# A first MLP's second product with tokens on the partitions, and queries and keys in wider matmuls

## The chip, the cores and the metric

The kernel runs on one core of a Trainium2 chip. The metric is the device time of one execution of the whole program, in microseconds (us). One core has TensorE (PE in the profile, with its weight loads shown apart as PEld), VectorE (DVE), ScalarE (ACT), GpSimdE (POOL) and DMA queues started from SyncE (SP). The kernel before was timed in three executions: 753.31 to 753.59 us, median 753.58 us.

## The reference

The input is 256 tokens of width 1024 in fp32. Two layers follow one another, each a mixer and an MLP with residual adds and RMS norms; the change touches the first layer's MLP and the second layer's mixer.

```python
def sq_relu_mlp(xn, w1, w2):                 # w1 1024 x 4096, w2 4096 x 1024
    return jnp.square(jax.nn.relu(xn @ w1)) @ w2

def odd_mixer(xn, w_in, w_o, cos_f, sin_f):  # second layer's mixer
    hcat = (xn @ w_in).reshape(b, s, DIL_GROUPS, 3, DIL_HEADS, HEAD_DIM)   # 3 groups, 16 heads of 64
    q = apply_rope(hcat[:, :, :, 0], cos_f, sin_f)
    k = apply_rope(hcat[:, :, :, 1], cos_f, sin_f)
    v = hcat[:, :, :, 2]
    return dilated_attention(q, k, v) @ w_o

for layer in range(DEPTH):                   # DEPTH = 2: even mixer, then odd mixer
    xn = rms_norm(x, norm_mix[layer])
    x = x + mixer(xn, ...)
    x = x + sq_relu_mlp(rms_norm(x, norm_mlp[layer]), mlp_w1[layer], mlp_w2[layer])
return rms_norm(x, norm_final)
```

`dilated_attention` takes, for each head, a softmax over the keys of each of three dilated windows, and combines the three by their softmax denominators.

## The kernel before

**Split products.** Every fp32 product is made of three matmuls. A tensor is split into a high part in the type fp32r (a cast on ACT, line 179) and the rest (a subtraction on DVE, line 180), and `mm3` (lines 182 to 185) multiplies high by high, high by low and low by high into one PSUM bank. The weights come by DMA into `raw` (4 buffers of 1 MB), are cast to `whi` on ACT and reduced to `wlo` on DVE (3 buffers each), and are used as the matmul's stationary or moving operand. The product can be issued in another form with fewer matmuls: `xT[2]`, called `xp` after the change, holds the high and the low part of x beside each other, so one matmul of 512 columns (the weights' high part against both) and one of 256 columns (the weights' low part against x's high part) give all three terms, in two halves of a bank that are added afterwards. The first product of both MLPs ("up", lines 347 and 348) is done so: ACT copies one half of the bank out (line 351), and DVE adds the other (line 352).

**Stages.** Four phases follow one another: the even mixer to about 137 us, the first MLP (`mlp_between`) to 297 us, the odd mixer (`odd`) to about 566 us, the second MLP (`finish`) to the end. Between them `hand_over` adds the result to x (line 297), multiplies by the norm's gains and splits the sum again (`prepare`, lines 218 to 220), block by block of two of the eight 128-wide slices of the width, while PE finishes the next block. x lies with the width on the partitions and the tokens along the row.

**First MLP.** 16 chunks of the hidden width are worked off, "up" three chunks ahead of "down". The second product, "down" (line 377, `onto` at line 305), has the weights stationary and the 256 tokens of the hidden activations (`hh`, `hl`) moving; its result lies as x does, in four banks. The squared activations carry the norm's scale squared, so the result is multiplied by one number for each token; since tokens lie along the row here, `inverse_row` (line 254) spreads that number over all partitions with a matmul, and line 295 multiplies by it on DVE. The second MLP's "down" (lines 397 to 405) has the activations stationary and 512 columns of weights moving; its result lies with the tokens on the partitions, where the scale is one number for each partition.

**Odd mixer.** It works in eight units of two heads. For each unit PE computes three blocks of queries and keys (`qk_steps`, blocks b = 0, 1, 2, each with two halves f for q and k over eight slices of the width, 48 matmuls of 256 columns) and the values (48 matmuls of 384 columns, line 815). The rotary embedding follows each block (`rope`, lines 841 to 857): four copies on ACT that swap halves of the rows out of PSUM into `sw` (lines 844 and 845), a product of the PSUM bank with the cosines on DVE (`r`, line 847), a product of `sw` with the sines (line 848), and an add. The attention of the unit before runs beside these steps (`attend`, `weave`): scores, softmax (DVE, ACT, DVE, ACT, lines 893 to 897), transposes of the probabilities (line 904) with copies out (line 906), and the product with the values, `mix` (lines 914 to 919), whose results are split into `mixed` (line 921).

**Order.** Instructions are put in order by a scheduler from the program order and priorities; `tc.high_priority` moves a step ahead. Each engine works in its own order and waits for semaphores. PSUM has eight banks, four under the tag "acc", four under the tag "w".

Of the kernel before, what the change touches and what calls it, by code (L numbers as in the profile page):

```python
# [23 lines left out]
P = 128  # L24
D = 1024
# [19 lines left out]
def trunk(ctx, tc, a, out):  # L45
# [9 lines left out]
    def scratch(shape, name):  # L55

        n = int(np.prod(shape))
        v = work.tile([P, 512], F32, tag="scratch", name=name, bufs=12)[:, :n]
        if len(shape) == 2:
            v = v.rearrange("p (a b) -> p a b", b=shape[1])  # L60
        return v

    def pair_tile():


        z = act.tile([P, KT, 2, T], F32R, tag="pair", name="pair", bufs=1)
        return z[:, :, 0, :], z[:, :, 1, :], z
# [7 lines left out]
    def bank(tag):  # L75
        return ps.tile([P, 512], F32, tag=tag, name=tag)
# [136 lines left out]
    def two(z):  # L213
        return z.rearrange("p (f n) -> p f n", f=2)
# [36 lines left out]
        nc.vector.reciprocal(inv, inv)  # L251
        return inv

    def inverse_row(s):

        pr = bank("w")
        nc.tensor.matmul(pr[:, 0:T], mean, s[:, 0:T], start=True, stop=True)
        inv = work.tile([P, T], F32, tag="inv", name="inv", bufs=1)
        nc.vector.tensor_scalar(inv, pr[:, 0:T], EPS, None, ALU.add)
        nc.vector.reciprocal(inv, inv)  # L260
        return inv

    def diagonal(r, t):
        dg = work.tile([P, P], F32, tag="diag", name="diag")
        nc.vector.tensor_scalar(dg, ident, r[:, t:t + 1], float(D), ALU.mult, ALU.mult)
# [12 lines left out]
    def sum_tile():  # L278
        return work.tile([P, 2 * T], F32, tag="squares", name="squares", bufs=1)
# [2 lines left out]
        for s in steps:  # L282
            s()

    def hand_over(accs, last, n, scale=None):

        xT = pair_tile()
        s = sum_tile()
        for b in range(4):
            last[b]()  # L290
            v, acc = x[:, 2 * b:2 * b + 2, :], two(accs[b])
            with tc.high_priority(NORM_PRIO):
                if scale is not None:
                    scaled = scratch([2, T], "scaled")
                    nc.vector.tensor_tensor(scaled, acc, scale.unsqueeze(1).broadcast_to([P, 2, T]), op=ALU.mult)
                    acc = scaled
                nc.vector.tensor_tensor(v, acc, v, op=ALU.add)
                for f in zip(*(prepare(k, n, xT) for k in (2 * b, 2 * b + 1))):
                    run_all(f)
        return xT, s  # L300

    def open_accs():
# [28 lines left out]
    def mlp(mp, xT, s, invert, tail, make_down, beside=lambda j: None):  # L331
# [39 lines left out]
            beside(j)  # L371
        return accs, hs, inv, {j: weight() for j in tail}

    def mlp_between(mp, xT, s):
        def down(accs, hs):
            def step(j, w, f, fbs=range(8)):
                onto(accs, w, f * D, (ALL, slice(f * T, f * T + T)), hs[j], (j, f) == (0, 0), (j, f) == (15, 1), fbs)
            return step

        accs, hs, inv, w = mlp(mp, xT, s, lambda: inverse_row(s), range(14, 16), down)  # L380

        def last(b):
            for j in w:
                for f in range(2):
                    down(accs, hs)(j, w[j], f, (2 * b, 2 * b + 1))

        return accs, [lambda b=b: last(b) for b in range(4)], inv

    def finish(mp, xT, s):

        HALF = [slice(0, 512), slice(512, D)]
        g = mp.tile([P, D], F32, name="gain")
        nc.sync.dma_start(g, a["norm_final"].partition_broadcast(P))
        xt = mp.tile([P, NT, D], F32, name="xt")
        tail = range(13, 16)

        def mm(acc, hs, j, w, f, t, c0, c1, first, last):
            tk, c = slice(f * T + t * P, f * T + (t + 1) * P), slice(f * D + c0, f * D + c1)
            mm3(acc, hs[j][0][:, tk], hs[j][1][:, tk], w[0][:, c], w[1][:, c], first, last)

        def down(accs, hs):
            def step(j, w, f):
# [374 lines left out]


    def odd(op, xT, s):
        xh, xl, _ = xT  # L780
        cosT = op.tile([P, T], F32, name="cosT")
        sinT = op.tile([P, T], F32, name="sinT")
        mask = op.tile([P, NT, 384], F32, name="mask")
# [42 lines left out]
        def qk_steps(d):  # L826


            hold = {}

            def gemm(b, f, half):
                if f == 0 and half == 0:
                    hold["w"], hold["p"] = weight(), bank("acc")
                (wh, wl), pq = hold["w"], hold["p"]
                for k in range(4 * half, 4 * half + 4):
                    ws = slice((f * KT + k) * P, (f * KT + k + 1) * P)
                    mm3(pq[:, f * T:(f + 1) * T], wh[:, ws], wl[:, ws], xh[:, k, :], xl[:, k, :], k == 0, k == KT - 1)
                if f == 1 and half == 1:
                    rope(b, pq)

            def rope(b, pq):
                sw, r1 = scratch([512], "sw"), scratch([2, T], "r1")
                for r in range(0, P, 64):
                    nc.scalar.copy(sw[r:r + 32], pq[r + 32:r + 64])  # L844
                    nc.scalar.copy(sw[r + 32:r + 64], pq[r:r + 32])  # L845
                sw = sw.rearrange("p (f n) -> p f n", f=2)
                nc.vector.tensor_tensor(r1, pq.rearrange("p (f n) -> p f n", f=2), cosT.unsqueeze(1).broadcast_to([P, 2, T]), op=ALU.mult)  # L847
                nc.vector.tensor_tensor(sw, sw, sinT.unsqueeze(1).broadcast_to([P, 2, T]), op=ALU.mult)  # L848
                if b == 0:
# [21 lines left out]
        def attention(u, d):  # L871
# [36 lines left out]
            def mix(out_tag):  # L908
                pvo = [bank(out_tag) for _ in range(NT)]
                for i in range(NT):  # L910
                    for kk in range(NT):
                        for j in range(2):
                            cs = slice(64 * j, 64 * j + 64)
                            nc.tensor.matmul(pvo[i][cs, 0:P], d["v0"][:, kk, cs], turned[i, j][:, kk, :], start=kk == 0, stop=False)
                    for c in range(2):
                        qs = slice(64 * c, 64 * c + 64)
                        for j in range(2):
                            cs = slice(64 * j, 64 * j + 64)
                            nc.tensor.matmul(pvo[i][cs, qs], d["v12"][:, 2 * i + c, cs], turned[i, j][:, 2, qs], start=False, stop=c == 1)
                for i in range(NT):  # L920
                    split(*(z[:, u % 4, tok(i)] for z in mixed[u // 4]), pvo[i][:, 0:P])

            return scores, [lambda v=(i, j): turn(*v) for i in range(NT) for j in range(2)], mix

# [46 lines left out]
    accs, last = phase("even", even)  # L971
    xT, s = hand_over(accs, last, 1)
    accs, last, scale = phase("mlp0", mlp_between, xT, s)
    xT, s = hand_over(accs, last, 2, scale)
    accs, last = phase("odd", odd, xT, s)
    xT, s = hand_over(accs, last, 3)
    phase("mlp1", finish, xT, s)
# [94 lines left out]
```

## Time and profile before

| | |
|---|---|
| median of three executions | 753.58 us (753.31 to 753.59) |
| the profiled execution | 753.46 us |
| its span (first to last instruction) | 751.7 us |
| granted TensorE clock over the span | 0.998 of full speed |
| PE busy | 741.5 us, 99 % |
| PEld (weight loads) busy | 680.8 us, 91 % |
| DVE busy | 523.4 us, 70 % |
| ACT busy | 512.3 us, 68 % |
| POOL busy | 8.7 us, 1 % |
| DMA | 172 GB/s on average |

Matmuls are pipelined, so the length that a matmul's row shows is longer than the distance to the next one. What a group of matmuls costs is read from the distance of their starts. A row of the timeline gives start and length, engine, line, operation, the written and read names, and the shape as partitions x elements of a row; brackets hold idle time before it and what ended it. A row of groups gives count, busy time in us and the mean length in ns, then the idle time before them.

### The profile page before, as it was taken

The page shows a single profiled execution, that of the slowest core. Times are in us where ns is not written, and L with a number is a line of the kernel's source. Part 1 is how long each engine was busy: PE and PEld are TensorE (multiplying, and loading weights), DVE is VectorE, ACT ScalarE, POOL GpSimd, SP SyncE. Part 2 cuts the span into 40 slices and gives each one's busy share as a digit, 9 for nine tenths or more (in the row PEclk, how much of TensorE's full clock was granted, in tenths as well). Part 3 has the DMA queues.
Part 4 walks back from the last instruction along what each step waited for, and adds up shares of the span by engine and source line. Part 5 has one row for each costly group of instructions (what it writes and reads, how often), then busy time and mean ns, then how long its engine had stood idle before and what let it go on. Part 6 is the DMA issues. An engine that isn't in the chain of part 4 may idle for free.

```text
span 751.7 us, 13661 instructions
## 1 busy us (share of the span) xinstructions
PE 741.5 (99%) x5385; PEld 680.8 (91%) x5385; DVE 523.4 (70%) x1089; ACT 512.3 (68%) x1111; POOL 8.7 (1%) x20
## 2 busy tenths in 40 slices
PE   9999999999999999999999999999999999999996
PEld 6998998999999999999999999999898888888885
DVE  6778858866566557886777676776858765666664
ACT  6788866554454455898988989889866554554551
POOL 0100000000000001000000000000000000000000
PEclk9999999999999999999999999999999999999999
DMA  8772334555554554544443434534555455555501
GB/s 290 306 267 99 116 114 163 182 212 171 176 214 168 174 191 148 211 154 142 168 148 148 155 143 172 189 117 159 205 197 168 172 221 177 187 195 176 196 22 56
DMA packets 22097, 129.08 MB, mean 172 GB/s; under 512 B 2705, under 2 KB 3729, under 8 KB 9233
## 3 DMA queue, kind: packets, MB, share of 16 engines
q1 hardware_dynamic: 21888, 127.95, 48.0%
q8 instruction: 42, 0.69, 0.4%
q10 hardware_dynamic: 144, 0.26, 0.1%
q14 instruction: 23, 0.18, 0.1%
HBM read 127.16 MB, written 1.05 MB: 171 GB/s over the span
## 4 chain that ended last, share of the span: by engine, by line
PE 66%; ACT 17%; DVE 10%; issue 4%; DMA 2%; SPq 0%; POOL 0%; POOLq 0%
PE w L347 16%; PE acc L183 12%; PE acc L184 12%; PE acc L185 12%; PE w L348 8%; ACT whi L179 6%; DVE wlo L180 4%; ACT sw L845 3%; ACT sw L844 3%; ACT v L822 1%; DVE r L847 1%; ACT pp L895 1%; DVE sw L848 1%; DVE k L857 1%; DVE sn L893 1%
## 5 line engine op out<-in xcount | busy, mean ns | idle before, releaser
L180 DVE TENSOR_TENSOR wlo<-raw,whi 128x512 fp32r<-128x512 f32 (+3 forms) x487 | 306.6, 662 | 146.2 <-ACT whi L179 145.8
L179 ACT CAST whi<-raw 128x512 fp32r<-128x512 f32 (+3 forms) x487 | 265.8, 601 | 144.9 <-PE w L347 62.4
L347 PE MATMUL w<-pair,whi 128*128 128x512 f32 x512 | 182.3, 398 | 0.0
L348 PE MATMUL w<-pair,wlo 128*128 128x256 f32 x512 | 143.9, 281 | 0.0
L183 PE MATMUL acc<-pair,whi 128*128 128x256 f32 x432 | 123.5, 286 | 0.0
L185 PE MATMUL acc<-pair,wlo 128*128 128x256 f32 x432 | 120.2, 278 | 0.0
L184 PE MATMUL acc<-pair,whi 128*128 128x256 f32 x432 | 120.0, 278 | 0.0
L347 PEld LDWEIGHTS w<-pair,whi 128*128 128x128 f32 x512 | 96.4, 188 | 22.9
L348 PEld LDWEIGHTS w<-pair,wlo 128*128 128x128 f32 x512 | 96.2, 188 | 0.5
L183 PEld LDWEIGHTS acc<-pair,whi 128*128 128x128 f32 x432 | 81.2, 188 | 1.3 <-issue 0.3
L185 PEld LDWEIGHTS acc<-pair,wlo 128*128 128x128 f32 x432 | 81.5, 189 | 0.0
L184 PEld LDWEIGHTS acc<-pair,whi 128*128 128x128 f32 x432 | 81.3, 188 | 0.0
L184 PE MATMUL acc<-hl,whi 128*128 128x256 f32 x256 | 72.5, 283 | 0.0
L185 PE MATMUL acc<-hh,wlo 128*128 128x256 f32 x256 | 72.5, 283 | 0.0
L183 PE MATMUL acc<-hh,whi 128*128 128x256 f32 x256 | 72.4, 283 | 0.0
L183 PEld LDWEIGHTS acc<-hh,whi 128*128 128x128 f32 x256 | 49.1, 192 | 0.6
L185 PEld LDWEIGHTS acc<-hh,wlo 128*128 128x128 f32 x256 | 49.0, 192 | 0.0
L184 PEld LDWEIGHTS acc<-hl,whi 128*128 128x128 f32 x256 | 49.0, 191 | 0.0
L183 PE MATMUL acc<-whi,hh 128*128 128x512 f32 x122 | 48.0, 393 | 0.0
L185 PE MATMUL acc<-whi,hl 128*128 128x512 f32 x122 | 47.6, 390 | 0.0
L184 PE MATMUL acc<-wlo,hh 128*128 128x512 f32 x122 | 47.6, 390 | 0.0
L184 PE MATMUL acc<-wlo,pair 128*128 128x384 f32 x128 | 44.0, 344 | 1.2 <-DVE wlo L180 1.1
(215 smaller groups left out, 1267.0 us busy)
## 6 DMA issues: line engine op xcount, KB each, us to landing
raw<-in_w SPq DMA_DIRECT2D x64, 1024.0 KB, 4.8
raw<-in_w_oqk SPq DMA_DIRECT2D x24, 1024.0 KB, 4.8
raw<-in_w_ov SPq DMA_DIRECT2D x16, 768.0 KB, 4.2
raw<-in_w_qk SPq DMA_DIRECT2D x4, 1024.0 KB, 9.9
raw<-in_w_oe SPq DMA_DIRECT2D x4, 1024.0 KB, 5.0
raw<-in_w_oo SPq DMA_DIRECT2D x4, 1024.0 KB, 4.9
bias<-in_rpb SPq DMA_DIRECT2D x8, 256.0 KB, 3.8
raw<-in_w_v SPq DMA_DIRECT2D x2, 512.0 KB, 6.7
```

The source lines that it names most:

```text
L179: a = nc.scalar.copy(hi, src).ins
L180: return a, (eng or nc.vector).tensor_tensor(lo, src, hi.bitcast(F32), op=ALU.subtract).ins
L183: nc.tensor.matmul(o, sh, mh, start=first, stop=False)
L184: nc.tensor.matmul(o, sh, ml, start=False, stop=False)
L185: nc.tensor.matmul(o, sl, mh, start=False, stop=last)
L347: nc.tensor.matmul(two(pu[f]), w[0][:, c], xT[2][:, k], start=k == 0, stop=False)
L348: nc.tensor.matmul(pu[f][:, 0:T], w[1][:, c], xT[0][:, k, :], start=False, stop=k == KT - 1)
L822: nc.scalar.activation(d["v12"][64:P, 2 * i + c, :], pq[rows, 2 * P:3 * P], AF.Copy, scale=ri[rows])
L844: nc.scalar.copy(sw[r:r + 32], pq[r + 32:r + 64])
L845: nc.scalar.copy(sw[r + 32:r + 64], pq[r:r + 32])
L847: nc.vector.tensor_tensor(r1, pq.rearrange("p (f n) -> p f n", f=2), cosT.unsqueeze(1).broadcast_to([P, 2, T]), op=ALU.mult)
L848: nc.vector.tensor_tensor(sw, sw, sinT.unsqueeze(1).broadcast_to([P, 2, T]), op=ALU.mult)
```

## The change

The first MLP's "down" takes the second MLP's form (`down_tokens`): activations stationary, 512 columns of weights moving. Its result then has the tokens on the partitions; the next stage needs the width there. `hand_over_tokens` therefore scales each bank on the way out (the first 256 columns on ACT, the others on DVE, one number for each partition), turns the 16 squares of 128 x 128 by transposes on PE into banks of the tag "w", and then adds and splits as before. `inverse_row` goes, `inverse_columns` takes its place.

In the second layer, queries and keys take the form of the "up" product: per block and half f, eight matmuls of 512 columns and eight of 256 columns into a bank of their own, which a reduce on DVE (`tensor_reduce` over two elements) adds into the tile `qk32` in SBUF. The rotary embedding reads that tile in place of PSUM. The splits that take the mixed values out of PSUM get the priority of the norm steps.

```diff
@@ hand_over becomes two functions; join is what both do to a block
+    def join(b, o, n, xT):
+        v = x[:, 2 * b:2 * b + 2, :]
+        nc.vector.tensor_tensor(v, two(o), v, op=ALU.add)
+        for f in zip(*(prepare(k, n, xT) for k in (2 * b, 2 * b + 1))):
+            run_all(f)
...
-                if scale is not None:
-                    scaled = scratch([2, T], "scaled")
-                    nc.vector.tensor_tensor(scaled, acc, scale.unsqueeze(1).broadcast_to([P, 2, T]), op=ALU.mult)
-                    acc = scaled
...
+    def hand_over_tokens(accs, last, n, scale):
+        xT, s = pair_tile(), sum_tile()
+        ys = {}
+        def leave(h, t):
+            last(h, t)
+            acc, sc = accs[2 * t + h], column(scale, t)
+            with tc.high_priority(NORM_PRIO):
+                y = ys[h, t] = scratch([512], "y")
+                nc.scalar.activation(y[:, 0:T], acc[:, 0:T], AF.Copy, scale=sc)
+                nc.vector.tensor_scalar(y[:, T:2 * T], acc[:, T:2 * T], sc, None, ALU.mult)
+        def turn(h):
+            with tc.high_priority(NORM_PRIO):
+                for b in range(2):
+                    pt = bank("w")
+                    for k in range(2):
+                        for t in range(NT):
+                            c = (2 * b + k) * P
+                            nc.tensor.transpose(pt[:, k * T + t * P:k * T + (t + 1) * P], ys[h, t][:, c:c + P], ident)
+                    join(2 * h + b, pt, n, xT)
+        leave(0, 0)
+        leave(0, 1)
+        leave(1, 0)
+        turn(0)
+        leave(1, 1)
+        turn(1)
+        return xT, s
@@ mlp_between
-            def step(j, w, f, fbs=range(8)):
-                onto(accs, w, f * D, (ALL, slice(f * T, f * T + T)), hs[j], (j, f) == (0, 0), (j, f) == (15, 1), fbs)
+            def step(j, w, f):
+                for i in range(4):
+                    down_tokens(accs[i], hs, j, w, f, i // 2, i % 2 * 512, i % 2 * 512 + 512, (j, f) == (0, 0), False)
...
-        accs, hs, inv, w = mlp(mp, xT, s, lambda: inverse_row(s), range(14, 16), down)
+        accs, hs, inv, w = mlp(mp, xT, s, lambda: inverse_columns(s), range(14, 16), down)
@@ odd, qk_steps
-                    hold["w"], hold["p"] = weight(), bank("acc")
-                (wh, wl), pq = hold["w"], hold["p"]
+                    hold["w"], hold["q"] = weight(), scratch([2, T], "qk32")
+                if half == 0:
+                    hold["p"] = bank("acc")
+                (wh, wl), pq, q32 = hold["w"], hold["p"], hold["q"]
                 for k in range(4 * half, 4 * half + 4):
                     ws = slice((f * KT + k) * P, (f * KT + k + 1) * P)
-                    mm3(pq[:, f * T:(f + 1) * T], wh[:, ws], wl[:, ws], xh[:, k, :], xl[:, k, :], k == 0, k == KT - 1)
+                    nc.tensor.matmul(two(pq), wh[:, ws], xp[:, k], start=k == 0, stop=False)
+                    nc.tensor.matmul(pq[:, 0:T], wl[:, ws], xh[:, k, :], start=False, stop=k == KT - 1)
+                if half == 1:
+                    nc.vector.tensor_reduce(q32[:, f], pq.rearrange("p (h n) -> p n h", h=2), axis=mybir.AxisListType.X, op=ALU.add)
                 if f == 1 and half == 1:
-                    rope(b, pq)
+                    rope(b, q32.rearrange("p f n -> p (f n)"))
@@ odd, mix
-                for i in range(NT):
-                    split(*(z[:, u % 4, tok(i)] for z in mixed[u // 4]), pvo[i][:, 0:P])
+                with tc.high_priority(NORM_PRIO):
+                    for i in range(NT):
+                        split(*(z[:, u % 4, tok(i)] for z in mixed[u // 4]), pvo[i][:, 0:P])
...
-    xT, s = hand_over(accs, last, 2, scale)
+    xT, s = hand_over_tokens(accs, last, 2, scale)
```

Around the first block of a unit, DVE had this order before (`drz` is a reciprocal of the softmax, `obl`/`oal` the low part of mixed values, `r` and `sw` the rotary products, `q0l` the low part of the first block's queries and keys):

```order
L896 RECIPROCAL drz<-dz 128x1
L180 TENSOR_TENSOR oal<-acc,oah 128x128
L896 RECIPROCAL drz<-dz 128x1
L180 TENSOR_TENSOR wlo<-raw,whi 128x384
L847 TENSOR_TENSOR r_4889<-acc,cosT 128x512
L848 TENSOR_TENSOR sw<-sw,sinT 128x512
L180 TENSOR_TENSOR wlo<-raw,whi 128x384
L850 TENSOR_TENSOR r_4889<-r_4889,sw 128x512
L180 TENSOR_TENSOR wlo<-raw,whi 128x384 x2
L180 TENSOR_TENSOR q0l<-r_4889,q0h 128x512
```

With the change (line 868 is the reduce, line 937 the copy out of a transposed block of probabilities, before on ACT):

```order
L927 RECIPROCAL drz<-dz 128x1
L868 TENSOR_REDUCE qk_4662<-acc 128x256
L927 RECIPROCAL drz<-dz 128x1
L868 TENSOR_REDUCE qk_4662<-acc 128x256
L180 TENSOR_TENSOR wlo<-raw,whi 128x384
L878 TENSOR_TENSOR r_4782<-qk_4662,cosT 128x512
L180 TENSOR_TENSOR wlo<-raw,whi 128x384
L937 COPY pts<-w 128x384
L879 TENSOR_TENSOR sw<-sw,sinT 128x512
L868 TENSOR_REDUCE qk_4804<-acc 128x256
L881 TENSOR_TENSOR r_4782<-r_4782,sw 128x512
L180 TENSOR_TENSOR wlo<-raw,whi 128x384 x2
```

The two reduces of the block stand between and behind the last reciprocals of the softmax, ahead of the product with the cosines, which no longer reads PSUM; the next block's first reduce stands ahead of the add of this block, and two of a unit's four copies `pts` have come over from ACT.

At the end of the first MLP, PE had the last triples of the "down" product and then the first value products of the odd mixer (`pair` is the split x):

```order
L183 MATMUL acc_1853<-hh_3267,whi_3391 128x256
L184 MATMUL acc_1853<-hl_3268,whi_3391 128x256
L185 MATMUL acc_1853<-hh_3267,wlo_3392 128x256
L183 MATMUL acc_1853<-hh_3385,whi_3451 128x256
L184 MATMUL acc_1853<-hl_3386,whi_3451 128x256
L185 MATMUL acc_1853<-hh_3385,wlo_3452 128x256
L183 MATMUL acc_1853<-hh_3385,whi_3451 128x256
L184 MATMUL acc_1853<-hl_3386,whi_3451 128x256
```

With the change, the last 512-column matmul is followed by value products, between which transposes of the scaled result `y` stand:

```order
L185 MATMUL acc_1855<-whi_3116,hl_3075 128x512
L183 MATMUL acc_3280<-whi_3128,pair_3139 128x384
L184 MATMUL acc_3280<-wlo_3129,pair_3139 128x384
L185 MATMUL acc_3280<-whi_3128,pair_3139 128x384
L183 MATMUL acc_3280<-whi_3128,pair_3139 128x384
L184 MATMUL acc_3280<-wlo_3129,pair_3139 128x384
L312 MATMUL w_3221<-ident_84,y_3218 128x128
L312 MATMUL w_3221<-ident_84,y_3183 128x128
L312 MATMUL w_3221<-ident_84,y_3218 128x128
L185 MATMUL acc_3280<-whi_3128,pair_3139 128x384
L183 MATMUL acc_3280<-whi_3128,pair_3139 128x384
L312 MATMUL w_3231<-ident_84,y_3218 128x128
```

Sixteen transposes have come in on PE there; the scheduler puts them in singly four times and in threes four times, among the last "down" matmuls and the first 24 value products.

## Rows read from the trace of the kernel before

**Rows 1.** five units of the second layer: stretch, length, busy PE, PEld, DVE, ACT
```profile
352.08:381.79 29.71, 29.71 (x265) 29.38 (x265) 20.63 (x46) 27.30 (x59) 0.00 (x0) 1.00 0.45 160
...
442.54:473.21 30.67, 30.35 (x265) 29.25 (x265) 21.60 (x48) 27.32 (x59) 0.00 (x0) 1.00 0.43 155
...
sum 151.79, PE 150.72 PEld 146.47 DVE 106.41 ACT 136.59 POOL 0.00; mean PE 30.14 PEld 29.30 DVE 21.28 ACT 27.32 POOL 0.00
```

**Rows 2.** timeline of PE, first MLP: start, length, line, names, shape
```profile
200.30 0.28 PE L183 MATMUL acc<-hh,whi 128*128 128x256 f32 x1
...
206.05 0.40 PE L347 MATMUL w<-pair,whi 128*128 128x512 f32 x1
...
211.70 0.28 PE L183 MATMUL acc<-hh,whi 128*128 128x256 f32 x1
```

**Rows 3.** timeline of PE, second MLP's second product, first and last start
```profile
650.67 0.39 PE L183 MATMUL acc<-whi,hh 128*128 128x512 f32 x1
...
656.14 0.39 PE L347 MATMUL w<-pair,whi 128*128 128x512 f32 x1
```

**Rows 4.** timeline of PE inside one unit of the second layer
```profile
422.92 0.28 PE L184 MATMUL acc<-pair,whi 128*128 128x256 f32 x1
...
425.54 0.49 PE L904 MATMUL w<-ident,pp 128*128 128x128 f32 x3
...
425.99 0.28 PE L184 MATMUL acc<-pair,whi 128*128 128x256 f32 x1
...
429.99 0.28 PE L185 MATMUL acc<-pair,wlo 128*128 128x256 f32 x1
```

**Rows 5.** waits of one engine, 297 to 575 us: total, times, longest
```profile
PEld acc L184 <- DVE wlo L180: 3.7, 9, 0.6
...
PE w L192 <- DVE obl L180: 0.6, 1, 0.6
...
DVE r L847 <- ACT sw L845: 34.8, 24, 3.2
```

**Rows 6.** value products of two units (instructions on the cast weights): length, busy
```profile
373.38:381.79 8.41, 8.24 (x32) 5.94 (x33) 3.49 (x7) 4.04 (x8) 1.00 0.37 142
...
464.03:473.21 9.18, 8.26 (x32) 5.95 (x33) 2.91 (x6) 4.26 (x8) 1.00 0.49 187
```

**Rows 7.** timeline of ACT through one unit
```profile
425.93 0.58 ACT L844 COPY sw<-acc 32x512 f32<-32x512 f32 x1
...
432.14 0.58 ACT L844 COPY sw<-acc 32x512 f32<-32x512 f32 x1
...
436.89 0.58 ACT L844 COPY sw<-acc 32x512 f32<-32x512 f32 x1
...
444.08 0.36 ACT L821 ACTIVATE v<-acc,rstd 64x128 f32<-64x128 f32 x1 [2.12 <-DVE v L818]
...
456.59 0.58 ACT L844 COPY sw<-acc 32x512 f32<-32x512 f32 x1
```

**Rows 8.** groups by line and shape: count, busy us, mean ns, idle before
```profile
L844 ACT COPY sw<-acc 32x512 f32<-32x512 f32 x48 | 27.8, 578 | 0.9
...
L179 ACT CAST whi<-raw 128x512 fp32r<-128x512 f32 x408 | 229.7, 619 | 137.4 <-PE w L347 62.4 <-PE acc L184 29.9 <-issue 20.2
...
L906 ACT COPY pts<-w 128x384 f32<-128x384 f32 x31 | 14.6, 479 | 0.8 <-PE w L904 0.2
...
L847 DVE TENSOR_TENSOR r<-acc,cosT 128x512 f32<-128x512 f32 x24 | 16.6, 692 | 34.8 <-ACT sw L845 34.8
...
L352 DVE TENSOR_TENSOR u<-w,side 128x256 f32<-128x256 f32 x64 | 26.9, 420 | 3.9 <-ACT side L351 3.6
...
L260 DVE RECIPROCAL inv<-inv 128x256 f32<-128x256 f32 x1 | 1.7, 1745 | 0.0
```

**Rows 9.** timelines of PE and DVE at the hand-over into the second layer
```profile
297.38 0.33 PE L183 MATMUL acc<-whi,pair 128*128 128x384 f32 x1
...
301.08 0.87 DVE L220 SCALAR_TENSOR_TENSOR pair<-gx,pair 128x256 fp32r<-128x256 f32 x2
```

More of the change, by code (lines that the diff above doesn't have):

```diff
@@ L252, in inverse_columns @@
         return inv
[L254 to L261, printed above, removed]
     def diagonal(r, t):
@@ L283, in run_all, with hand_over @@
             s()
-    def hand_over(accs, last, n, scale=None):
-        xT = pair_tile()
-        s = sum_tile()
+    def join(b, o, n, xT):
[3 more added lines that the diff above has]
+            run_all(f)
+    def hand_over(accs, last, n):
+        xT, s = pair_tile(), sum_tile()
         for b in range(4):
             last[b]()
-            v, acc = x[:, 2 * b:2 * b + 2, :], two(accs[b])
             with tc.high_priority(NORM_PRIO):
-                if scale is not None:
-                    scaled = scratch([2, T], "scaled")
-                    nc.vector.tensor_tensor(scaled, acc, scale.unsqueeze(1).broadcast_to([P, 2, T]), op=ALU.mult)
-                    acc = scaled
-                nc.vector.tensor_tensor(v, acc, v, op=ALU.add)
-                for f in zip(*(prepare(k, n, xT) for k in (2 * b, 2 * b + 1))):
-                    run_all(f)
+                join(b, accs[b], n, xT)
+        return xT, s
+    def hand_over_tokens(accs, last, n, scale):
+        xT, s = pair_tile(), sum_tile()
+        ys = {}
[21 more added lines that the diff above has]
+        turn(1)
         return xT, s
@@ L372, in mlp, with down_tokens, last @@
         return accs, hs, inv, {j: weight() for j in tail}
+    HALF = [slice(0, 512), slice(512, D)]
+    def down_tokens(acc, hs, j, w, f, t, c0, c1, first, last):
+        tk, c = slice(f * T + t * P, f * T + (t + 1) * P), slice(f * D + c0, f * D + c1)
+        mm3(acc, hs[j][0][:, tk], hs[j][1][:, tk], w[0][:, c], w[1][:, c], first, last)
     def mlp_between(mp, xT, s):
         def down(accs, hs):
-            def step(j, w, f, fbs=range(8)):
-                onto(accs, w, f * D, (ALL, slice(f * T, f * T + T)), hs[j], (j, f) == (0, 0), (j, f) == (15, 1), fbs)
-            return step
-        accs, hs, inv, w = mlp(mp, xT, s, lambda: inverse_row(s), range(14, 16), down)
-        def last(b):
+            def step(j, w, f):
+                for i in range(4):
+                    down_tokens(accs[i], hs, j, w, f, i // 2, i % 2 * 512, i % 2 * 512 + 512, (j, f) == (0, 0), False)
+            return step
+        accs, hs, inv, w = mlp(mp, xT, s, lambda: inverse_columns(s), range(14, 16), down)
+        def last(h, t):
             for j in w:
                 for f in range(2):
-                    down(accs, hs)(j, w[j], f, (2 * b, 2 * b + 1))
-        return accs, [lambda b=b: last(b) for b in range(4)], inv
+                    down_tokens(accs[2 * t + h], hs, j, w[j], f, t, h * 512, h * 512 + 512, False, (j, f) == (15, 1))
+        return accs, last, inv
     def finish(mp, xT, s):
-        HALF = [slice(0, 512), slice(512, D)]
         g = mp.tile([P, D], F32, name="gain")
@@ L395, in finish @@
         tail = range(13, 16)
-        def mm(acc, hs, j, w, f, t, c0, c1, first, last):
-            tk, c = slice(f * T + t * P, f * T + (t + 1) * P), slice(f * D + c0, f * D + c1)
-            mm3(acc, hs[j][0][:, tk], hs[j][1][:, tk], w[0][:, c], w[1][:, c], first, last)
+        mm = down_tokens
         def down(accs, hs):
@@ L779, in odd @@
     def odd(op, xT, s):
-        xh, xl, _ = xT
+        xh, xl, xp = xT
         cosT = op.tile([P, T], F32, name="cosT")
```

## The prediction, made before the changed kernel ran

> **What bounds the kernel now.** I read the table of busy times first. PE is busy 741.5 of 751.7 us, so almost everything is the distance between starts of matmuls, and what I need is that distance for each shape that goes and each that comes. I read it from the timeline of PE. In the first MLP, the 48 matmuls of 256 columns between 200.30 and 206.05 take 5.75 us, 0.1198 us each; the 32 matmuls of the up product behind them, 16 pairs of 512 and 256 columns, take 5.65 us, 0.353 us a pair [rows 2]. In the second MLP, 24 matmuls of 512 columns take 5.47 us, 0.228 us each [rows 3]. In the second layer the query and key matmuls of 256 columns run at two rates: 23 intervals in the 2.62 us from 422.92, 0.1139 us each, and 34 in the 4.00 us from 425.99, 0.1176 us each; between them lie three transposes and one matmul of 256 columns in 0.45 us, which leaves 0.335 us for the three [rows 4].
>
> Then I read the busy times by unit, since there PE is not alone. The first steady unit is 29.71 us long and PE is busy in all of it; the later ones are 30.67 us with PE busy 30.35 [rows 1]. Their value products show why: 8.41 us in an early unit, 9.18 us in a late one, for the same 48 matmuls [rows 6]. The waits name the low part of the weights on DVE: 3.7 us in nine waits of PE's weight loads [rows 5]. ACT is busy 27.3 and DVE 21.6 us of the unit [rows 1], so neither is full, but they wait for one another: the cosine product on DVE waits 34.8 us for ACT's copies, over all blocks [rows 5]. The timeline of ACT shows the loop that results. The copies of one unit's three blocks start at 425.93, 432.14 and 436.89, the copies out of the values at 444.08, the next unit's first block at 456.59, 30.66 us later [rows 7]. That chain sets the late units; PE sets the early ones and the MLPs.
>
> **The change, part by part.**
>
> *First MLP's second product.* 768 matmuls of 256 columns become 384 of 512. By the distances above, 768 x 0.1198 = 92.0 us become 384 x 0.228 = 87.5 us: **-4.5 us**. The least gain is at the up product's rate, where two thirds of a pair's 0.353 are 0.235 a matmul: 90.4, -1.6 us. I take **-4.4**, as the second MLP issues this very form.
>
> *Hand-over.* 16 transposes come onto PE, in four threes at 0.335 us and four single ones. The three in rows 4 hold 0.24 us of start distances and some 0.095 us of restart, an estimate from where the next matmul starts; a single one is then 0.175 us. 4 x 0.335 + 4 x 0.175 = **+2.0 us**. The multiplication by the token's scale moves from DVE into the copies out, and the reciprocal over 256 columns (1.745 us, once, [rows 8]) becomes one over two; neither lies on PE's path, nothing. Before, the last split of this hand-over ended at 301.95, 4.57 us after the first value product at 297.38 [rows 9], and PE needs the second half of x after 24 value products, 24 x 0.175 = 4.2 us (rate from [rows 6]: 8.41 / 48). With eight transposes among them that is 5.2 us. The chain after the last matmul: y on ACT and then on DVE (about 0.42 us each, as the 256 columns from PSUM of [rows 8]), three transposes, then for two blocks an add (0.69) and two low parts (0.87 together in [rows 9]): 0.84 + 0.34 + 3.1 = 4.3 us. It fits; I take no stall. If the cover fails, it costs up to 1.5 us.
>
> *Queries and keys, PE.* A unit's 144 matmuls become 48 pairs. At the up product's rate 48 x 0.353 = 16.9 us. Before, with 98 of the 144 at the faster of the two rates and 46 at the slower, counted along the unit of rows 4, it was 98 x 0.1139 + 46 x 0.1176 = 16.6: **+0.4 us** a unit. So PE's own need is 29.7 + 0.4 = 30.1 us. If the pair ran at the faster rate, it would be 3 x 0.1139 = 0.342 and the need unchanged.
>
> *Queries and keys, DVE and ACT.* Each half of a block gets a reduce, six a unit. The trace has none. It reads 512 numbers a partition from PSUM and writes 256: below lies 0.42 us (an add of 256 from PSUM), beside it 0.692 us (the product over 512 from PSUM), above 1.745 us (a reciprocal of 256) [rows 8]. I take 0.69, the row with its amount of reading. The cosine product gets its operand from SBUF and no longer shares a bank with ACT's copies; before, it started after them. That takes 0.69 us off the loop where it stood behind the copies. Two of the four copies of transposed probabilities (0.479 us on ACT, [rows 8]) move to DVE. In all, on the loop: between the first and the second block's copies +0.25 (a reduce in, a product out of it); second to third nothing; from the third to the values -1.4 (product parallel to the copies, and the copy moved); to the next unit +0.55. From 30.66 that gives 30.1, and with ends of 29.3 and 30.5 for the copies' own time I take **30.3**.
>
> A bank is also held until its reduce is done, and there are six of them a unit now, out of four buffers that the mixed and the value products share. The first half of the third block takes the bank of the first block's first half. Its matmul comes about 5.5 us before the values, which start 21.5 us into the unit (464.03 after 442.54, [rows 1, 6]), so at 16.0. The reduce stands behind the softmax's reciprocals, ahead of the cosine product, and the copies before that started 14.05 us into the unit (456.59 after 442.54, [rows 1, 7]); with 0.7 us for the reduce that leaves 1.2 us. No wait.
>
> *Priority of the mixed values.* The casts come earlier on ACT, so the banks are free earlier. The single wait of the last product for them, 0.6 us [rows 5], goes: **-0.6**. What stands behind the casts on ACT is the softmax's scaling; two casts of 128 columns delay it by less than a `pts` copy each, once a unit; this is in the 30.3.
>
> *Second layer in all.* First two units' queries and keys: +0.8, as PE sets them. The five units, 151.79 us [rows 1]: the first becomes 30.1, four 30.3, 151.3, so -0.5. The last unit -0.1, the wait -0.6. Together **-0.4**.
>
> **Sum**: -4.4 + 2.0 - 0.4 = -2.8. The profiled execution took 753.46 us, its span 751.7 and 1.76 around it, which stays. 750.7; the median lies 0.12 above that execution: **750.8 us**.
>
> Two rules of the Trainium skill bear on this. Its page "TensorE: Matmul & The Clock Gate", section "Back-to-back issue gap", gives 262 cycles for 256 columns and 518 for 512 as the isolated gap, and says that the distance in a real stream is set by the load and the matmul together. By its gaps a pair would cost 0.325 us, against 0.353 in rows 2, so the trace does not agree for the pair; by the rule 48 pairs would be 15.6 us a unit. The page "VectorE: DVE Perf Modes", section "The TRN2 errata — SBUF-src ops pay a fixed extra latency per instruction", speaks against the change: it gives ScalarE 52 cycles more (43 ns, an estimate) for a copy from SBUF than for one from PSUM, and the rotary copies move from PSUM to SBUF. Rows 8 bear it out in sign.
>
> **The rivals.**
>
> *1. The pairs run at the faster rate.* For it: PE's weight loads are busy 29.38 of 29.71 us in a unit [rows 1], and the change takes 48 of a unit's loads away. Against: the up product has the very pair at 0.353 [rows 2]. The pair at 0.342 leaves PE's need at 29.7; the loop of 30.1 then decides. Five units 29.7 + 4 x 30.1 = 150.1, -1.7; the first two 0; the last -0.5; the wait -0.6: -2.8 and so 748.4 us; with the loop at 29.3 as well, 746.
>
> *2. The reduce is long (slower).* At 1.2 us, half-way to the bound, each reduce ahead of the cosine product lengthens the loop by 0.5 us at two or three places of the unit: 31.6. Five units 30.1 + 4 x 31.6 = 156.5, +4.7; first two and last +2.4; wait -0.6: +6.5, so 753.58 + 4.1 = 757.7 us. At the bound, DVE itself would be full: 21.6 + 6 x 1.745 + 2 x 0.48 = 33.0 us a unit, 764 us. It decides from about 0.9 us a reduce. For it: nothing in the trace bounds it from above but the reciprocal. Against: its reading is that of the row at 0.692.
>
> *3. The hand-over is exposed.* The last transposes stand five to ten value products behind the last matmul, and y needs two engines one after the other, as the cosine product waits for the copies of its bank [rows 5]. 1.5 us late gives 752.3 us.
>
> *4. The copies from SBUF are slower.* The nearest rows: 0.619 us for a cast of 512 columns from SBUF against 0.578 for the copy from PSUM [rows 8], 0.04 us, twelve of them a unit: +0.5. The loop is then 30.6. Five units 152.5, +0.7; the first two +0.8; the last +0.2; the wait -0.6: +1.1, and 752.3 us.
>
> **How the numbers follow.** Chances: forecast 0.45 (its own range 749 to 752.5, from the rate of the first part and the ends of the loop), rival 1 0.18, rival 2 0.12, rivals 3 and 4 0.13 and 0.12. The range 746 to 756.5 takes in rival 1 and the nearer part of rival 2 and leaves out less than 2 in 10. A measurement of this kernel tells 0.2 %, 1.5 us, from no change, so "faster" ends at 752.1. Faster: most of the forecast, rival 1, and a few of 3 and 4, 0.65. Same: most of 3 and 4, and the forecast's upper end, 0.23. Slower: rival 2, 0.12.
>
> **What would show it.** In the profile after: the 512-column matmuls of the first MLP 0.228 us apart; the pairs in the second layer at 0.353 or 0.342; a reduce of about 0.69 us; units of 30.3 us, the value products without the wait for low weights where PE sets the unit; no wait of PE for y, the transposed bank or a reduce's bank. Units above 30.7 us, or weight loads that wait longer for DVE than 3.7 us, would make the forecast wrong, as would 512-column matmuls at 0.235.

## The result and the profile after

The changed kernel takes 755.14 us (754.83 to 755.65, 16 runs); the kernel before took 753.62 us beside it (753.07 to 754.81). The ratio is 1.0018, interval 1.0011 to 1.0026: 1.5 us slower, where 2.8 us faster was forecast (750.8 us). The profiled execution took 755.53 us, its span 753.7. On the page PE's busy time is as before, its weight loads are fewer, and DVE has 32 us more:

```profile
PE 741.1 (98%) x4635; PEld 646.4 (86%) x4635; DVE 555.5 (74%) x1149; ACT 511.3 (68%) x1103; POOL 8.7 (1%) x20
```

The timeline of PE in the first MLP, in answer to [rows 2, 3]; 24 matmuls of 512 columns lie between the two starts, 5.47 us, 0.228 each, as the forecast took it:

```profile
198.50 0.39 PE L183 MATMUL acc<-whi,hh 128*128 128x512 f32 x1
...
203.97 0.39 PE L368 MATMUL w<-pair,whi 128*128 128x512 f32 x1
```

At the hand-over, in answer to [rows 9], the first value product starts at 294.20 us and not at 297.38. Threes of transposes stand among the value products, and queries start at 303.42 us, 2.28 us earlier than before (305.70). The forecast for the first MLP with its hand-over was -2.4:

```profile
294.20 0.34 PE L183 MATMUL acc<-whi,pair 128*128 128x384 f32 x1
...
295.13 0.55 PE L312 MATMUL w<-ident,y 128*128 128x128 f32 x3
...
303.42 0.39 PE L865 MATMUL acc<-pair,whi 128*128 128x512 f32 x1
```

So the time is lost behind 303 us. The busy times by unit (stretch, length, then PE, PEld, DVE, ACT, POOL with counts), in answer to [rows 1]:

```profile
350.74:380.76 30.02, 30.02 (x218) 27.44 (x217) 25.96 (x55) 25.74 (x54) 0.00 (x0) 1.00 0.40 142
...
442.41:473.71 31.30, 30.54 (x217) 27.42 (x217) 26.17 (x56) 26.73 (x57) 0.00 (x0) 1.00 0.43 152
...
sum 154.28, PE 151.89 PEld 137.13 DVE 129.68 ACT 132.68 POOL 0.00; mean PE 30.38 PEld 27.43 DVE 25.94 ACT 26.54 POOL 0.00
```

The first of these five units is PE's own length, 30.02 us (30.1 was forecast), and the second is 30.33 us long. The other three, the late units, are 31.3 us, where 30.67 was before and 30.3 forecast. The five together are 2.5 us longer than before, and the last unit's queries and keys (505.02 to 527.91 us, 22.89 us against 21.55) another 1.3. The stretch ahead of the five, with the first two units' queries and keys, is 0.9 us longer (0.8 was forecast), and the stretch behind 527.91 us 0.5 shorter; with the 2.28 us that gives the 2.0 us between the two spans. What PE shows is in its timeline in a late unit and in the waits of its weight loads between 294 and 577 us (total, times, longest):

```profile
449.34 0.39 PE L865 MATMUL acc<-pair,whi 128*128 128x512 f32 x1
...
451.46 0.40 PE L865 MATMUL acc<-pair,whi 128*128 128x512 f32 x1
...
452.68 0.50 PE L865 MATMUL acc<-pair,whi 128*128 128x512 f32 x1 [0.71 <-DVE oal L180]
```

```profile
PEld acc L865 <- DVE oal L180: 2.5, 3, 1.0
PEld acc L865 <- DVE obl L180: 2.1, 2, 1.0
```

Six pairs take 2.12 us, 0.353 each, as the forecast took it. Then the next half block waits for a PSUM bank that the mixed values of the unit before still hold (`oal`, `obl` are their low parts, and the bank is free when these have been taken out of it). The values no longer wait, 8.41 us, in answer to [rows 6]:

```profile
465.30:473.71 8.41, 8.23 (x32) 5.94 (x33) 3.06 (x5) 2.80 (x5) 1.00 0.45 168
```

That suggests a reading in which the bank is the cause. The timeline of ACT suggests another one, in answer to [rows 7]:

```profile
443.62 0.36 ACT L847 ACTIVATE v<-acc,rstd 64x128 f32<-64x128 f32 x1 [2.52 <-DVE v L844]
...
457.17 0.62 ACT L875 COPY sw<-qk 32x512 f32<-32x512 f32 x1
...
463.78 0.62 ACT L875 COPY sw<-qk 32x512 f32<-32x512 f32 x1 [0.28 <-DVE qk L868]
...
468.72 0.62 ACT L875 COPY sw<-qk 32x512 f32<-32x512 f32 x1 [0.47 <-DVE qk L868]
...
474.91 0.36 ACT L847 ACTIVATE v<-acc,rstd 64x128 f32<-64x128 f32 x1 [2.52 <-DVE v L844]
```

From the first block's copies to the second's it is 6.61 us, to the third's 4.94, from there to the values 6.19, and from the values to the next unit's first copies 13.55, where before it was 6.21, 4.75, 7.19 and 12.51. ACT's copies now wait for DVE's reduces. The groups that matter, in answer to [rows 8], DVE's wait for the copies, in answer to [rows 5] (34.8 us before), and the shares of the chain of waits over two late units, first after, then before (percent of 64 us; the lines of shares are cut at their end):

```profile
L868 DVE TENSOR_REDUCE qk<-acc 128x256 f32<-128x512 f32 x48 | 32.7, 683 | 0.3 <-PE acc L866 0.3
...
L875 ACT COPY sw<-qk 32x512 f32<-32x512 f32 x48 | 29.7, 618 | 5.2 <-DVE qk L868 4.7
...
L937 DVE COPY pts<-w 128x384 f32<-128x384 f32 x13 | 7.2, 551 | 0.0
```

```profile
DVE sw L879 <- ACT sw L876: 7.5, 14, 0.9
```

```profile
by line: DVE wlo L180 23.6%; ACT sw L876 7.8%; ACT sw L875 7.7%; DVE qk L868 7.5%; ACT whi L179 6.5%; DVE sw L879 6.4%; DVE sn L924 5.8%; DVE k L888 5.3%; issue 4.9%; ACT v L848 4.6%; ACT v L847 3.6%; ACT pp L928 2.7%; ACT pp L926 2.2%; DVE
```

```profile
by line: ACT whi L179 20.4%; DVE wlo L180 12.6%; ACT sw L845 9.2%; ACT sw L844 9.1%; issue 8.7%; DVE k L857 6.4%; ACT v L822 4.5%; DVE r L847 4.3%; ACT pp L895 4.1%; ACT v L821 4.1%; DVE sw L848 3.7%; ACT pts L906 3.0%; DVE sn L893 2.9%; AC
```

The chain goes round a late unit on the two engines alone; among its pieces there is none of PE, before or after. Added up piece by piece over one late unit, DVE had 10.2 of its 30.67 us and ACT 18.4 before; now DVE has 19.4 of 31.3 and ACT 11.2. This round of work, in which each engine waits for the other and which ends where the next unit's begins, is called the loop below. Theory 1 says that the banks cause the 31.3 us, theory 2 that this loop does and PE's wait is where PE catches up with it.

### The profile page after: what moved, and what is told of

Its sections match the earlier page's. It is cut to its first block, busy times and chain, and to the rows that moved or that the text cites. A ratio compares the mean times of both kernels' runs of the same rounds, so it can differ in the third digit from the quotient of the medians.

```text
span 753.7 us, 12208 instructions
## 1 busy us (share of the span) xinstructions
PE 741.1 (98%) x4635; PEld 646.4 (86%) x4635; DVE 555.5 (74%) x1149; ACT 511.3 (68%) x1103; POOL 8.7 (1%) x20
## 4 chain that ended last, share of the span: by engine, by line
PE 65%; DVE 16%; ACT 12%; DMA 3%; issue 3%; SPq 1%; POOL 0%; POOLq 0%; ACTq 0%
PE w L368 16%; PE acc L183 11%; PE acc L185 11%; PE acc L184 11%; PE w L369 8%; DVE wlo L180 6%; ACT sw L876 3%; ACT sw L875 2%; ACT whi L179 2%; DVE qk L868 2%; DVE sw L879 2%; PE acc L865 2%; DVE sn L924 1%; DVE k L888 1%; ACT v L848 1%
## 5 line engine op out<-in xcount | busy, mean ns | idle before, releaser
L865 PE MATMUL acc<-pair,whi 128*128 128x512 f32 x384 | 140.7, 405 | 3.1 <-DVE oal L180 1.4
L183 PE MATMUL acc<-whi,hh 128*128 128x512 f32 x250 | 98.1, 393 | 0.0
L185 PE MATMUL acc<-whi,hl 128*128 128x512 f32 x250 | 97.7, 391 | 0.0
L184 PE MATMUL acc<-wlo,hh 128*128 128x512 f32 x250 | 97.7, 391 | 0.0
L865 PEld LDWEIGHTS acc<-pair,whi 128*128 128x128 f32 x384 | 72.2, 188 | 21.9 <-DVE oal L180 2.5
L185 PEld LDWEIGHTS acc<-whi,hl 128*128 128x128 f32 x250 | 47.0, 188 | 9.9
L183 PEld LDWEIGHTS acc<-whi,hh 128*128 128x128 f32 x250 | 47.0, 188 | 9.9
L184 PEld LDWEIGHTS acc<-wlo,hh 128*128 128x128 f32 x250 | 47.0, 188 | 8.8
L183 PE MATMUL acc<-whi,pair 128*128 128x384 f32 x128 | 43.8, 342 | 0.0
L185 PE MATMUL acc<-whi,pair 128*128 128x384 f32 x128 | 43.1, 337 | 0.0
L875 ACT COPY sw<-qk 32x512 f32<-32x512 f32 x48 | 29.7, 618 | 5.2 <-DVE qk L868 4.7
L868 DVE TENSOR_REDUCE qk<-acc 128x256 f32<-128x512 f32 x48 | 32.7, 683 | 0.3 <-PE acc L866 0.3
```

Of the source, the lines that this page charges most:

```text
L183: nc.tensor.matmul(o, sh, mh, start=first, stop=False)
L184: nc.tensor.matmul(o, sh, ml, start=False, stop=False)
L185: nc.tensor.matmul(o, sl, mh, start=False, stop=last)
L865: nc.tensor.matmul(two(pq), wh[:, ws], xp[:, k], start=k == 0, stop=False)
L868: nc.vector.tensor_reduce(q32[:, f], pq.rearrange("p (h n) -> p n h", h=2), axis=mybir.AxisListType.X, op=ALU.add)
```

## The experiments

In each, the kernel before ran beside it on the same chip (753.2 to 753.4 us). Rows of stretches are to be read as those of the units above.

**The parts one at a time.** Each of two kernels has one part of the change: the first MLP with its hand-over, or the second layer's.

```diff
-    xT, s = hand_over(accs, last, 2, scale)
+    xT, s = hand_over_tokens(accs, last, 2, scale)     # and mlp_between as changed; odd as before
```

> Only the first MLP's second product by token and its hand-over; queries, keys and the mixed values' splits as before. In the trace of the change the second layer starts its value products 3.2 us earlier and its query products 2.3 us earlier than before. If the two parts of the change add up, this kernel is 2.3 us faster than the one before (751.3 us), and units of the second layer stay at 30.67 us. Rival: the loop of the second layer takes the gain back, because it starts with less slack; then it is within 1 us of the one before.

750.9 us, ratio 0.9967 (0.9955 to 0.9980).

> Only the second layer's part (pairs of matmuls, reduce, priority of the splits); first MLP as before. If the parts add up: +4.3 us, 757.9 us, with late units of 31.3 us and the same waits of PE for the mixed values' bank. Rival: the longer units come from the state that the new hand-over leaves behind; then units stay near 30.7 us and the time near 754 us.

757.8 us, ratio 1.0063 (1.0049 to 1.0076). One late unit of each:

```profile
439.54:470.21 30.67, 30.36 (x265) 29.30 (x265) 21.59 (x48) 27.34 (x59) 0.00 (x0) 1.00 0.45 156
```

```profile
444.20:475.50 31.30, 30.56 (x217) 27.42 (x217) 26.17 (x56) 26.73 (x57) 0.00 (x0) 1.00 0.44 152
```

That is -2.3 and +4.6 us; their sum, 2.3, differs from the whole change's 1.5 by less than the intervals, of about 1 us to either side each, can tell. The first part does what was forecast, and the second, forecast at -0.4, loses 4.6 by itself, whatever stands ahead of it.

**One bank for the mixed values.**

```diff
-                pvo = [bank(out_tag) for _ in range(NT)]
+                pv = bank(out_tag)
+                pvo = [pv[:, i * P:(i + 1) * P] for i in range(NT)]
```

> The change, but both mixed-value products of a unit go into one PSUM bank, so a unit takes nine banks of the four in turn and not ten; no work is added or taken away. Theory 1 (PSUM banks: PE waits 1.08 us a late unit for a bank that the mixed values hold, and that alone makes units 31.3 us): the wait goes or shrinks, units come to 30.2 us, 751 us. Theory 2 (VectorE and ScalarE form a loop of 31.3 us by themselves, since VectorE got 4.1 us of reduces a unit between ScalarE's copies; PE's wait for the bank is only where PE catches up with it): units stay at 31.3 us, the wait shows up at another place (the values' weights, the next unit's scores), 755 us.

761.18 us, ratio 1.0102 (1.0089 to 1.0116). A late unit, and all that PE's weight loads wait for in it:

```profile
442.51:474.10 31.59, 30.24 (x218) 27.38 (x218) 26.13 (x56) 26.85 (x57) 0.00 (x0) 1.00 0.45 150
```

```profile
PEld w L935 <- ACT pp L928: 1.7, 1, 1.7
PEld w L192 <- issue: 0.3, 1, 0.3
```

The wait for the bank is gone, the unit is no shorter, and PE waits at another place, for the softmax. Theory 1, by which the unit had to shrink with that wait, falls. The edit did not take away the wait alone, though: in the trace the splits of the mixed values stand behind further softmax steps on both engines, and the unit is 0.3 us longer. The further 5 us are lost behind the units: from the last unit's value products to the end it takes 231.0 us, against 225.8 in the change, with one stop of PE of 3.5 us (1.1 there) and a lower clock behind it (last section).

**A shorter reduce.** One half of the bank is copied and the sum of the two halves is left out.

```diff
-                    nc.vector.tensor_reduce(q32[:, f], pq.rearrange("p (h n) -> p n h", h=2), axis=mybir.AxisListType.X, op=ALU.add)
+                    nc.vector.tensor_scalar(q32[:, f], pq[:, 0:T], 1.0, None, ALU.mult)
```

> The change, but the reduce reads only one half of the bank (a copy of 256 columns, the sum of the two halves is left out), so VectorE does about 0.27 us less six times a unit, 1.6 us, and everything else is as in the change, banks too. Theory 2 (loop of VectorE and ScalarE): late units fall from 31.3 by most of the 1.6 us until PE's own 30.2 us bounds them, 750.5 to 752 us. Theory 1 (banks): the bank of the mixed values comes free at the same place in the order behind the softmax, units stay above 31 us, 754 to 755 us.

753.1 us, ratio 0.9998 (0.9989 to 1.0007); a late unit, the group in place of the reduce, and the chain's shares over that unit:

```profile
441.42:472.38 30.96, 30.27 (x217) 27.42 (x217) 24.60 (x56) 26.71 (x57) 0.00 (x0) 1.00 0.45 153
```

```profile
L868 DVE TENSOR_SCALAR qk<-acc 128x256 f32<-128x256 f32 x48 | 19.9, 416 | 0.3
```

```profile
by line: DVE wlo L180 23.2%; ACT sw L876 10.1%; ACT sw L875 10.1%; issue 7.8%; DVE sw L879 6.7%; ACT whi L179 6.7%; DVE sn L924 6.0%; ACT v L848 4.7%; DVE k L888 4.4%; ACT v L847 3.6%; DVE qk L868 3.3%; ACT pp L928 2.8%; ACT pp L926 2.3%; D
```

Neither number was met: 1.6 us less on DVE gave 0.35 us a unit. The chain shows where most of the rest went: ACT's rotary copies grew from 15.5 % of it (over the two units above) to 20.2, 5.0 to 6.3 us a unit, and the time in which no wait is seen (issue) from 4.9 to 7.8 %. In that part of the unit the two engines are nearly level, and most of what one gives, the other takes.

**The priority.** The splits of the mixed values without `tc.high_priority` in the change, and with it in the kernel that has the first MLP's part alone.

> The change without the priority of the mixed values' splits. The prediction gave the priority 0.6 us, once. Theory 1 (banks): the splits come later, PE waits longer for their bank, late units grow beyond 31.3 us, over 757 us. Theory 2 (loop of VectorE and ScalarE): the same work stands in another order on the two engines, a late unit changes by no more than 0.3 us either way, 754 to 757 us.

755.68 us, ratio 1.0035 (1.0021 to 1.0048); a late unit is 31.32 us long, though PE's weight loads now wait up to 1.4 us at a time for the bank, where it was 1.0:

```profile
443.18:474.50 31.32, 30.28 (x218) 27.43 (x218) 26.12 (x56) 26.73 (x57) 0.00 (x0) 1.00 0.43 151
```

That is what theory 2 expected. The pieces of the chain over this unit are 15.7 us of DVE and 14.9 of ACT, against 19.4 and 11.2 in the change, at the same length: two ways round that are nearly equally long.

> The first MLP's part and the priority of the mixed values' splits, queries and keys as before. By the prediction the priority is worth 0.6 us once: 750.3 us. By the loop: the splits' places on ScalarE and VectorE move by one or two instructions, 750.5 to 751.3 us.

751.78 us, ratio 0.9980 (0.9972 to 0.9989), a late unit 30.89 us. The 0.6 us were not gained. If anything the priority costs here, which is not shown: the interval overlaps that of 0.9967 without it.

**Part of the subtractions on GpSimd**, in the change and in the first MLP's part alone.

```diff
+        if odd_lo <= j < odd_hi and i == 3:
+            eng = nc.gpsimd
         return split(hi, lo, raw, eng)
```

> The change, but in the second layer the last of the four low-part subtractions of every weight chunk runs on GpSimd, which is idle there, so VectorE does 2.8 us less a unit (three of 0.6 us, two of 0.47 us). Theory 2 (loop): units fall from 31.3 to 30.2 to 30.6 us, near PE's own need, 750.5 to 752.5 us. Theory 1 (banks): the mixed values' splits stand behind the same softmax on ScalarE, so the wait for their bank stays and units stay above 31 us, 754 to 755 us. A third way: GpSimd's subtraction is so slow, or slows VectorE so much, that weights come late; then PE waits for them, and it is slower than 755 us.

772.17 us, ratio 1.0256 (1.0242 to 1.0270).

> The first MLP's part of the change alone, with the same subtractions on GpSimd. Without them it took 750.9 us, with late units of 30.67 us and a loop of ScalarE and VectorE in which ScalarE has 18 and VectorE 10 us. Theory 2: units fall toward PE's 29.7 us, 747 to 750 us. If VectorE's work does not count in this loop, since ScalarE's does: 750.5 to 751 us. If GpSimd is too slow: over 751 us.

765.28 us, ratio 1.0160 (1.0146 to 1.0174). Both went the third way, so they say nothing on the theories. The groups in the first of the two kernels:

```profile
L184 POOL TENSOR_TENSOR wlo<-raw,whi 128x512 fp32r<-128x512 f32 x24 | 44.3, 1846 | 94.7 <-ACT whi L183 63.6 <-DVE v L848 24.0 <-PE acc L869 4.5
```

```profile
L885 DVE TENSOR_TENSOR r<-r,sw 128x512 f32<-128x512 f32 x8 | 11.1, 1383 | 0.2
```

GpSimd takes 1.25 to 1.83 us for what DVE does in 0.69 (the mean of 1.85 has the first, of 6.16 us, in it), and the add on DVE that falls beside it takes 1.38 us as a mean of eight in place of 0.68.

**Work taken off ScalarE.** Two copies for the rotary swap in place of four, which exchange the two heads and leave out the exchange of the halves within each; or the four as DMAs.

```diff
-                    nc.scalar.copy(sw[r:r + 32], pq[r + 32:r + 64])
-                    nc.scalar.copy(sw[r + 32:r + 64], pq[r:r + 32])
+                    nc.scalar.copy(sw[r:r + 64], pq[64 - r:P - r])
```

> The change, but ScalarE makes two copies of 64 rows for each block's rotary swap and not four of 32 rows (the two heads are swapped instead of the halves within a head), 2 x 0.62 us less a block, 3.7 us less a unit; banks, reduces and their order stay. Theory 2 (loop of ScalarE and VectorE): the copies are 4.96 us of the loop in the trace; without half of them it falls below PE's own need and units are 30.2 us, PE's wait for the mixed values' bank goes, 750.5 to 751.5 us. Theory 1 (too few banks in themselves): the bank of the mixed values is released behind the softmax as before, the wait of about 0.9 us stays and units are 31 us or more, 754.5 to 755.5 us.

747.86 us, ratio 0.9930 (0.9916 to 0.9943). A late unit, the longest waits of PE's weight loads from 303 to 570 us, and two groups:

```profile
440.23:470.25 30.02, 30.02 (x218) 27.43 (x218) 25.15 (x54) 24.00 (x54) 0.00 (x0) 1.00 0.46 158
```

```profile
PEld w L192 <- issue: 2.0, 8, 0.3
PEld w L263 <- DVE diag L256: 0.4, 1, 0.4
```

```profile
L875 ACT COPY sw<-qk 64x512 f32<-64x512 f32 x48 | 29.8, 620 | 0.9
L936 ACT COPY pts<-w 128x384 f32<-128x384 f32 x31 | 14.6, 475 | 2.3 <-PE w L934 2.2
```

A copy of 64 rows takes as long as one of 32 (0.620 and 0.618 us), so the edit takes 3.7 us a unit off ACT. Banks and reduces are those of the change. The scheduler did more than the edit, however: the two copies `pts` that the change had put on DVE are on ACT again, and both engines' order is another, so that ACT has 2.7 us less a unit and DVE 1.0 (25.15 and 26.17). With less work on the two engines the unit is PE's own 30.02 us, and no wait for the bank is left. Theory 2 is shown from this side, for the two engines together; what the copies alone did is not separated from the rest. The time lies below what was expected, which came from the units alone: from the end of the seventh unit's values to the end it is 245.8 us against 248.7 in the change, another 2.9.

> The change, but the rotary swap, which now reads SBUF, is made by four small DMAs a block from SyncE's queue instead of four copies on ScalarE: 7.4 us less a unit on ScalarE. Theory 2: units at PE's 30.2 us, 750.4 us, if the DMAs land within about 3 us. Rival: their landing, or the weight loads that wait behind them in SyncE's queue, takes the copies' place in the loop, and units stay above 31 us, 755 us or more.

747.41 us, ratio 0.9922 (0.9909 to 0.9934), with the full computation: units of 30.02 us, ACT at 20.19 us of them, and the DMAs land in 2.0 us. Here too the `pts` copies are all on ACT again, and DVE has 25.14 us:

```profile
440.38:470.40 30.02, 30.02 (x218) 27.43 (x217) 25.14 (x54) 20.19 (x48) 0.00 (x0) 1.00 0.56 184
```

```profile
sw<-qk SPq DMA_DIRECT2D x96, 64.0 KB, 2.0
```

**The old form without the loop.** The first MLP's part alone, queries and keys as before, with two or all four of a unit's copies `pts` on VectorE (the line shown is the one for all four).

```diff
-                nc.any.tensor_copy(out=pts, in_=pt[:, 0:384].rearrange("p (b n) -> p b n", b=3))
+                nc.vector.tensor_copy(out=pts, in_=pt[:, 0:384].rearrange("p (b n) -> p b n", b=3))
```

> The first MLP's part alone, and two of a unit's four copies of transposed probabilities on VectorE instead of ScalarE (0.95 us less on ScalarE, in whose part of the old loop they stand with 0.95 us). By theory 2, applied to the kernel before (18.4 us of its loop are ScalarE's), late units fall from 30.67 to 29.7 to 30.1 us: 747.5 to 749.5 us. If the copies only go from one side of the loop to the other: 750.5 to 751 us.

748.18 us, ratio 0.9931 (0.9919 to 0.9943); late units are 29.7, then 30.26 us.

> As the one before it, with all four copies on VectorE. By theory 2 late units at PE's 29.7 us, 747 to 748.5 us, unless VectorE becomes the longer side, then 750 to 752 us.

745.91 us, ratio 0.9900 (0.9887 to 0.9914): the fastest of these kernels, 7.5 us below the kernel before. Units are PE's 29.70 us to the last:

```profile
438.71:468.41 29.70, 29.70 (x266) 29.37 (x265) 23.27 (x53) 25.62 (x55) 0.00 (x0) 1.00 0.45 161
```

## Why the prediction was wrong

**The step that failed** is "Queries and keys, DVE and ACT", the sum over the loop: "From 30.66 that gives 30.1 [...] I take 30.3". It measured 31.3, and the prediction's own sign, units above 30.7 us, came. The terms, each as forecast and then as the timeline of ACT shows it: first to second block +0.25 and +0.40; second to third nothing and +0.19; third to the values -1.4 and -1.0; on to the next unit +0.55 and +1.04. All four missed to the same side, 1.2 us in sum. The sum took ACT's chain of before, a stretch at a time, and named one reduce in it, while four of the six reduces (7.5 % of 64 us, 2.4 us a unit) came to stand on the loop, and the chain went over to DVE's queue. There more of the low parts of the weights, which had in part run beside ACT, are on the path: 23.6 % of it, where it was 12.6. The three late units, with the last unit's queries and keys, account for 3.0 + 1.4 = 4.4 us, against 4.3 between forecast and result. How the 1.2 us divide among the reduces, the order on DVE and the slower copies stays open: with each of the six reduces 0.27 us shorter, only 0.35 us a unit came back.

**Rival 2 had the place, and the wrong price.** It made the loop decide only from a reduce of about 0.9 us on; the reduce takes 0.683 us, as the forecast took it (0.69), and the loop was the bound already.

**"That leaves 1.2 us. No wait."** That was worked out for the reduce's bank and holds: PE waits for no reduce. But the same ring also holds the mixed values, which come free behind the softmax, about 10 us into the unit, and for these the sum was not made; PE waits there, 0.87 us between starts. It costs nothing by itself: with the wait gone (one bank less) a unit was no shorter, and with a longer one (without the priority) no longer.

**Right, with the trace:** 512 columns at 0.228 us, the pair at 0.353, PE's own unit 30.02 (30.1), the hand-over without a stall beyond some tenths, -2.28 for the first part (-2.4). So rivals 1 and 3 did not occur. Rival 4 did, in size (0.618 against 0.578 us, its 0.04), as one part of the loop's growth. Not right: the 0.6 us for the priority. The wait that it was to take away, of the last unit's scores for a bank, is still there, 1.1 us where it was 0.6.

That the pair costs PE more than the three matmuls also stands: 30.02 against 29.70 us in units in which PE is busy throughout, 0.32 a unit where 0.4 was forecast.

## What to carry to other kernels

Where two engines hand work to each other round a loop that is as long as the bound, an edit to either cannot be priced by its own instructions: write down the whole new round, each engine in its own order, and ask which queue the round goes through now. A wait of PE for a buffer can say where PE caught up with the loop, and not that the buffers are too few; test it by taking away the wait and, apart from it, work of the engines behind it, and look in the trace at what else the edit moved. Here fewer weight loads on PE bought nothing in the second layer, and moving four copies a unit to the emptier engine bought 5 us beyond the first MLP's part.

## What the runs showed of the hardware

While GpSimd ran a subtraction with two inputs in SBUF, an add of two SBUF tensors on DVE took twice its time (1.383 us as a mean of 8, seven of them at 1.47 to 1.52 and one at 0.69; 0.683 in the change). The Trainium skill, page "SBUF — State Buffer", section "Terms", says that these two engines share a pair of ports, held for a whole instruction by one while the other is blocked; the trace agrees, with 0.7 us. The first subtraction on GpSimd, by contrast, took 6.16 us (from 299.79 us), beside a run of subtractions and adds on DVE at their usual 0.68; there it was not DVE that was held up.

The kernel with one bank for the mixed values shows the granted clock after PE's stop (busy 1.67 of 5 us): 0.81 of full speed, then 0.51, the lower of the two levels (1.2 of 2.4 GHz) for nearly all of the stretch, then full again.

```profile
540.00:545.00 5.00, 1.67 (x13) 1.48 (x15) 3.78 (x9) 4.32 (x12) 0.00 (x0) 0.81 0.76 239
545.00:550.00 5.00, 5.00 (x30) 4.67 (x27) 4.21 (x14) 4.73 (x12) 0.00 (x0) 0.51 0.60 211
550.00:555.00 5.00, 5.00 (x46) 5.00 (x45) 1.07 (x3) 2.66 (x7) 0.00 (x0) 1.00 0.44 182
```

From 546.74 to 549.51 us the matmuls of 256 columns start 0.213 us apart, from 550.74 on 0.114. PE was at the lower level from the end of the stop at 543.33 to about 549.7 us, so that the stop costs some 3 us beyond its own length, an estimate from these distances.
